# Thresholded attention: two heads per step in a hand-ordered software pipeline, with paired loads and a ones column in V

## The chip, the cores and the metric

One core of one Trainium2 chip. The metric is the device time of one execution in microseconds (us). Runs within 1.5% of the fastest of the same kernel on the same chip are called fast, and ratios use fast runs alone.

## The reference

Batch 8, 12 heads, 512 positions, head size 64, all fp32, threshold 0.1:

```python
scores = einsum('bhqd,bhkd->bhqk', Q, K) * scale
weights = exp(scores - max(scores))
weights = weights / (sum(weights) + 1e-10)
weights = where(weights > threshold, weights, 0)
weights = weights / (sum(weights) + 1e-10)
return einsum('bhqk,bhkd->bhqd', weights, V)
```

Both kernels leave out the maximum, and compare exp(score) with 0.1 times the sum of its row rather than divide first. So a row needs two sums: that of all exps (for the threshold) and that of the exps kept (for the division at the end).

## The kernel before

Per batch it loads Q, K and V whole, repacks Q and K on ScalarE so that two heads lie side by side (128 columns), and transposes each pair, so that the even head of a pair lies on partitions 0 to 63 and the odd one on 64 to 127. Then it goes head by head, and in each head by tiles of 128 queries, which I call slices; there are 8 x 12 x 4 = 384. The order on the engines is left to the scheduler.

```python
for hp in range(HP):                                   # repacking
    nc.scalar.mul(q_dst[:, hp], q_src[:, hp], 1.0)
    nc.scalar.mul(k_dst[:, hp], k_src[:, hp], 1.0)
...                                                    # cut: fp32 transposes of pairs, copied out by ScalarE
for h in range(H):
    pslc = slice(h2 * 64, (h2 + 1) * 64)               # cut: h2 = h % 2
    ...
    for qi in range(SO):
        nc.tensor.matmul(sc[:], lhsT=qt_h[:, qi, :], rhs=kt_h, start=True, stop=True)
        nc.scalar.activation(exp_sb[:], sc[:], Exp, scale=scale, accum_out=sum1[:])
        nc.vector.tensor_scalar_mul(tv[:], sum1[:], thr)
        nc.vector.scalar_tensor_tensor(                # the mask
            out=masked[:], in0=exp_sb[:], scalar=tv[:], in1=exp_sb[:],
            op0=is_gt, op1=mult, accum_out=sum2[:])
        nc.vector.tensor_scalar_add(sum2[:], sum2[:], 1e-10)
        nc.vector.reciprocal(rcp2[:], sum2[:])
        for kj in range(SO):                           # cut: four bf16 transposes, masked -> pt_ps
        nc.vector.tensor_copy(pt_sb[:], pt_ps[:])
        for kj in range(SO):                           # cut: four value matmuls, pt_sb x v -> ops
        nc.vector.tensor_scalar_mul(out_sb[:, h, qi, :], ops[:], rcp2[:])
```

The softmax here doesn't subtract the row's maximum and nothing guards it: scores larger than these inputs give would overflow.

## Time and profile before

| kernel before | value |
|---|---|
| time, three runs | 711.37 us median (699.3 to 713.16) |
| busy share: TensorE, VectorE, ScalarE | 94%, 81%, 51% |
| one slice on TensorE, undisturbed | 1.50 us |
| stretches at half clock | 24 us from about 169; 3.4 us three times; from about 664 to the end |

In the profile lines PE is TensorE, PEld its loading of weights, DVE VectorE, ACT ScalarE and POOL GpSimd; L104 is a line of the kernel. The prediction below reads the engine shares, the chain (the work that ended last, followed back) and TensorE's timeline.

### The profile page before, as it was taken

What the parts mean: (1) busy time and instruction counts of PE and PEld (TensorE: products, weight loads), DVE (VectorE), ACT (ScalarE), POOL (GpSimd) and SP (SyncE); (2) the same over time, 40 slices, a digit from 0 to 9 for tenths busy, and PEclk for the clock granted to TensorE, in tenths of its full rate; (3) what the DMA queues carried; (4) which work ended last, traced back from release to release, by engine and by line L of the source; (5) the groups of instructions that cost most, each with busy time, mean ns of one, the idle gap of its engine ahead of it and who ended that gap; (6) DMA issues with size and microseconds to landing.
All of it is one profiled execution on the core that took longest, in us unless ns stands there. A gap on an engine that the chain in (4) does not pass through costs nothing.

```text
span 710.7 us, 12702 instructions
## 1 busy us (share of the span) xinstructions
PE 669.9 (94%) x4224; PEld 313.0 (44%) x4224; DVE 576.8 (81%) x2696; ACT 363.9 (51%) x961; POOL 1.1 (0%) x8
## 2 busy tenths in 40 slices
PE   2999999999999999999999999999999999999993
PEld 1544454443454445344454445444454444444442
DVE  0588898887588889888898989888898898888664
ACT  5663458443385346843476445844476345544320
POOL 0000000000000000000000000000000000000000
PEclk9999999997599999999999999999999999999655
DMA  9750006500055000730047000650023000200002
GB/s 304 228 178 1 1 2 190 167 1 1 1 178 178 2 1 14 246 98 1 1 130 227 1 2 1 188 168 1 1 69 111 1 1 1 90 0 1 1 0 90
DMA packets 49730, 51.14 MB, mean 72 GB/s; under 512 B 512, under 2 KB 49664, under 8 KB 49664
## 3 DMA queue, kind: packets, MB, share of 16 engines
q1 hardware_dynamic: 49664, 50.33, 22.3%
q8 instruction: 33, 0.54, 0.3%
q14 instruction: 33, 0.27, 0.1%
HBM read 37.75 MB, written 12.58 MB: 71 GB/s over the span
## 4 chain that ended last, share of the span: by engine, by line
PE 86%; DVE 5%; ACT 4%; issue 3%; DMA 2%; ACTq 0%; SPq 0%
PE sc L104 56%; PE pt_ps L125 14%; PE ops L133 9%; PE ps L90 7%; ACT exp_sb L107 3%; DVE out_sb L135 2%; DMA k_sb<-in_K_dram 2%; DVE masked L115 1%; DVE pt_sb L130 1%; ACT k_hp L82 1%; ACT qt L92 1%; DVE rcp L122 0%; DVE sum L121 0%; ACT q_hp L81 0%; DVE tv L112 0%
## 5 line engine op out<-in xcount | busy, mean ns | idle before, releaser
L104 PE MATMUL sc<-kt,qt 64*128 64x512 f32 x768 | 446.0, 675 | 11.6 <-ACT exp_sb L107 10.7
L107 ACT ACTIVATE exp_sb<-sc 128x512 f32<-128x512 f32 x384 | 229.4, 597 | 307.0 <-DVE masked L115 160.5
L115 DVE SCALAR_TENSOR_TENSOR masked<-exp_sb,tv 128x512 bf16<-128x512 f32 x384 | 282.1, 740 | 0.2
L130 DVE COPY pt_sb<-pt_ps 128x512 bf16<-128x512 bf16 x384 | 158.7, 414 | 45.3 <-PE pt_ps L125 43.3
L125 PE MATMUL pt_ps<-identity_bf,masked 128*128 128x128 bf16 x1536 | 163.9, 229 | 2.7 <-DVE masked L115 1.8
L125 PEld LDWEIGHTS <-masked 128*128 128x128 bf16 x1536 | 98.9, 101 | 150.2 <-DVE sum L121 82.6
L135 DVE TENSOR_SCALAR out_sb<-ops,rcp 128x64 f32<-128x64 f32 x384 | 108.2, 282 | 58.2 <-PE ops L133 52.8
L133 PEld LDWEIGHTS <-pt_sb 128*128 128x128 bf16 x1536 | 78.6, 100 | 165.3 <-DVE rcp L122 41.7
L104 PEld LDWEIGHTS sc<-kt,qt 64*128 64x128 f32 x768 | 116.5, 193 | 51.9 <-ACT exp_sb L107 19.9
L133 PE MATMUL ops<-v_bf,pt_sb 128*128 128x64 bf16 x1536 | 112.8, 198 | 3.8 <-DVE pt_sb L130 1.0
L107 ACT ACTIVATION_READ_ACCUMULATOR exp_sb<-sc 128x1 f32 x384 | 75.2, 196 | 0.0
L122 DVE RECIPROCAL rcp<-sum 128x1 f32<-128x1 f32 x384 | 59.4, 155 | 0.1
L121 DVE TENSOR_SCALAR sum<-sum 128x1 f32<-128x1 f32 x384 | 54.7, 143 | 0.0
L90 PE MATMUL ps<-identity_f,q_hp 128*128 128x128 f32 x192 | 38.2, 300 | 11.2 <-ACT q_hp L81 8.6
L112 DVE TENSOR_SCALAR tv<-sum 128x1 f32<-128x1 f32 x384 | 39.5, 143 | 6.4 <-ACT exp_sb L107 6.4
L90 PE MATMUL ps<-identity_f,k_hp 128*128 128x128 f32 x192 | 33.9, 292 | 4.5 <-ACT k_hp L82 3.3
L92 ACT ACTIVATE qt<-ps 128x512 f32<-128x512 f32 x48 | 28.6, 597 | 13.7 <-PE ps L90 8.2
L81 ACT ACTIVATE q_hp<-q_sb 128x512 f32<-128x512 f32 x48 | 29.4, 625 | 5.8 <-DMA q_sb<-in_Q_dram 5.8
L115 DVE DVE_READ_ACCUMULATOR masked<-exp_sb,tv 128x1 f32 x384 | 31.7, 82 | 0.0
L90 PEld LDWEIGHTS ps<-identity_f,q_hp 128*128 128x128 f32 x192 | 22.5, 149 | 17.6 <-issue 11.6
L92 ACT ACTIVATE kt<-ps 128x512 f32<-128x512 f32 x48 | 28.5, 594 | 2.8 <-PE ps L90 2.8
L82 ACT ACTIVATE k_hp<-k_sb 128x512 f32<-128x512 f32 x48 | 29.5, 625 | 0.8 <-DMA k_sb<-in_K_dram 0.8
(11 smaller groups left out, 40.0 us busy)
## 6 DMA issues: line engine op xcount, KB each, us to landing
q_sb<-in_Q_dram SPq DMA_DIRECT2D x8, 1536.0 KB, 7.1
k_sb<-in_K_dram SPq DMA_DIRECT2D x8, 1536.0 KB, 10.7
v_sb<-in_V_dram SPq DMA_DIRECT2D x8, 1536.0 KB, 10.1
out_dram<-out_sb SPq DMA_DIRECT2D x8, 1536.0 KB, 6.9
```

Source lines behind the costliest of these rows:

```text
L90: nc.tensor.matmul(ps[:, r, :], lhsT=src[:, hp, r, :], rhs=identity_f32[:], is_transpose=True, start=True, stop=True)
L92: nc.scalar.mul(dst[:, hp, :, :], ps[:], 1.0)
L104: nc.tensor.matmul(sc[:], lhsT=qt_h[:, qi, :], rhs=kt_h, start=True, stop=True)
L107: nc.scalar.activation(exp_sb[:], sc[:], mybir.ActivationFunctionType.Exp, scale=scale, accum_out=sum1[:],)
L112: nc.vector.tensor_scalar_mul(tv[:], sum1[:], thr)
L115: nc.vector.scalar_tensor_tensor(out=masked[:], in0=exp_sb[:], scalar=tv[:], in1=exp_sb[:], op0=mybir.AluOpType.is_gt, op1=mybir.AluOpType ...
L121: nc.vector.tensor_scalar_add(sum2[:], sum2[:], 1e-10)
L122: nc.vector.reciprocal(rcp2[:], sum2[:])
L125: nc.tensor.matmul(pt_ps[:, kj, :], lhsT=masked[:, kj * P:(kj + 1) * P], rhs=identity_bf[:], is_transpose=True, start=True, stop=True)
L130: nc.vector.tensor_copy(pt_sb[:], pt_ps[:])
L133: nc.tensor.matmul(ops[:], lhsT=pt_sb[:, kj, :], rhs=v_h[:, kj, :], start=(kj == 0), stop=(kj == SO - 1))
L135: nc.vector.tensor_scalar_mul(out_sb[:, h, qi, :], ops[:], rcp2[:])
```

## The change

The unit becomes a group: one tile of 128 queries of both heads of a pair. There are 192 groups, four to a pair of heads, 48 pairs.

- Both scores of a group are issued one right behind the other. Their operands lie on partitions 0 to 63 and 64 to 127, so they use two row groups of the array.
- V gets a 65th column of ones, so that the value matmul also gives the sum of the exps kept. The mask needs no accumulator, and add, reciprocal and scaling are done once per pair.
- The threshold product and the cast of V go to GpSimd. Half of the copies of transposed probabilities, now of 1024 columns, go to ScalarE.
- Q and K are loaded pair by pair straight into the paired layout, four pairs ahead. ScalarE's repacking goes; the pieces of Q and K in DRAM shrink from 1 KB to 256 bytes.
- Every instruction stays in program order (`keep`), and the program order is a pipeline: scores of group g, transposes of g-2, value matmuls of g-3.

```diff
+    def paired(ap):
+        return ap.rearrange("b (hp h2) (p r) d -> (b hp) p r h2 d", h2=2, p=P, r=SO)
+    keep = tc.keep_in_program_order
...
+        v_one = consts.tile([P, 2, SO, DV], bf16, name=f"v_one{i}")
+        nc.gpsimd.memset(v_one[:, :, :, D:DV], 1.0)
...
-        for hp in range(HP):
-            nc.scalar.mul(q_dst[:, hp], q_src[:, hp], 1.0)
-            nc.scalar.mul(k_dst[:, hp], k_src[:, hp], 1.0)
...
+    def do_qk(g):
+        hp, qi = divmod(g, SO)
+        for h2 in range(2):
+            sc = spsum.tile([P, SO * P], f32)
+            ps = slice(h2 * D, (h2 + 1) * D)
+            keep(nc.tensor.matmul(sc[:], lhsT=q_t[hp][ps, qi * P:(qi + 1) * P],
+                                  rhs=k_t[hp][ps, :], start=True, stop=True))
...
-                nc.vector.tensor_scalar_mul(tv[:], sum1[:], thr)
+        keep(nc.gpsimd.tensor_scalar(tv[:], sum1[:], thr, 1.0, op0=ALU.mult, op1=ALU.mult))
...
-                    accum_out=sum2[:],
-                nc.vector.tensor_scalar_add(sum2[:], sum2[:], 1e-10)
-                nc.vector.reciprocal(rcp2[:], sum2[:])
...
+    def do_out(hp):                       # once per pair
+        keep(nc.vector.tensor_scalar_add(rcp[:], ops[:, :, :, D:DV]..., 1e-10))
+        keep(nc.vector.reciprocal(rcp[:], rcp[:]))
+        for h2 in range(2):
+            keep(nc.vector.tensor_tensor(out=out_sb[:, h2], in0=ops[:, h2, :, 0:D],
+                in1=rcp[:, h2, :].unsqueeze(2).to_broadcast([P, SO, D]), op=ALU.mult))
...
+    for g in range(G + 4):                # conditions for the first and last groups cut
+        do_qk(g)
+        do_pt(g - 2)
+        tr = do_tr(nxt, "q" if qi == 1 else "k")     # in two groups of four
+        do_pv(g - 3)
+        do_exp(g)
+        do_trev(nxt, "q" if qi == 1 else "k", tr)
+        do_mask(g - 1)
+        do_ptev(g - 2, "act" if g % 2 else "dve")
+        do_out((g - 3) // SO)                        # at the end of a pair
```

More of the change, by code (lines that the diff above doesn't have):

```diff
@@ L5 @@
 from concourse import bass_utils, mybir
-from concourse.masks import make_identity
 from concourse._compat import with_exitstack
@@ L25 @@
     HP = H // 2
+    NP = B * HP
+    DV = D + 1
     scale = 1.0 / float(D) ** 0.5
@@ L29 @@
     bf16 = mybir.dt.bfloat16
+    ALU = mybir.AluOpType
+    keep = tc.keep_in_program_order
     def flat(ap):
-        return ap.rearrange("b h (p r) d -> b p h r d", p=P, r=SO)
-    Qf = flat(Q); Kf = flat(K); Vf = flat(V); Of = flat(out)
+        return ap.rearrange("b (hp h2) (p r) d -> (b hp) p h2 r d", h2=2, p=P, r=SO)
+    def paired(ap):
+        return ap.rearrange("b (hp h2) (p r) d -> (b hp) p r h2 d", h2=2, p=P, r=SO)
+    Qf, Kf, Vf, Of = paired(Q), paired(K), flat(V), flat(out)
     consts = ctx.enter_context(tc.tile_pool(name="consts", bufs=1))
-    identity_bf = consts.tile([P, P], bf16)
-    nc.gpsimd.memset(identity_bf[:], 0.0)
-    nc.gpsimd.affine_select(
-        out=identity_bf[:], in_=identity_bf[:],
-        compare_op=mybir.AluOpType.not_equal, fill=1.0,
-        base=0, pattern=[[-1, P]], channel_multiplier=1,
-    )
     identity_f32 = consts.tile([P, P], f32)
@@ L47 @@
         out=identity_f32[:], in_=identity_f32[:],
-        compare_op=mybir.AluOpType.not_equal, fill=1.0,
+        compare_op=ALU.not_equal, fill=1.0,
         base=0, pattern=[[-1, P]], channel_multiplier=1,
     )
-    load_pool = ctx.enter_context(tc.tile_pool(name="load", bufs=1))
-    cast_pool = ctx.enter_context(tc.tile_pool(name="cast", bufs=1))
-    t_pool = ctx.enter_context(tc.tile_pool(name="t", bufs=1))
-    tpsum = ctx.enter_context(tc.tile_pool(name="tpsum", bufs=2, space=bass.MemoryType.PSUM))
-    spsum = ctx.enter_context(tc.tile_pool(name="spsum", bufs=2, space=bass.MemoryType.PSUM))
+    identity_bf = consts.tile([P, P], bf16)
+    nc.gpsimd.tensor_copy(identity_bf[:], identity_f32[:])
+    NV = 3
+    v_bufs = []
+    for i in range(NV):
+        v_one = consts.tile([P, 2, SO, DV], bf16, name=f"v_one{i}")
+        nc.gpsimd.memset(v_one[:, :, :, D:DV], 1.0)
+        v_bufs.append(v_one)
+    load = ctx.enter_context(tc.tile_pool(name="load", bufs=6))
+    tpool = ctx.enter_context(tc.tile_pool(name="t", bufs=3))
+    spsum = ctx.enter_context(tc.tile_pool(name="spsum", bufs=4, space=bass.MemoryType.PSUM))
     ptpsum = ctx.enter_context(tc.tile_pool(name="ptpsum", bufs=2, space=bass.MemoryType.PSUM))
@@ L59 @@
     work = ctx.enter_context(tc.tile_pool(name="work", bufs=4))
-    small = ctx.enter_context(tc.tile_pool(name="small", bufs=16))
-    outp = ctx.enter_context(tc.tile_pool(name="out", bufs=2))
-    for b in range(B):
-        q_sb = load_pool.tile([P, H, SO, D], f32)
-        k_sb = load_pool.tile([P, H, SO, D], f32)
-        v_sb = load_pool.tile([P, H, SO, D], f32)
-        nc.sync.dma_start(out=q_sb[:], in_=Qf[b])
-        nc.sync.dma_start(out=k_sb[:], in_=Kf[b])
-        nc.sync.dma_start(out=v_sb[:], in_=Vf[b])
-        v_bf = cast_pool.tile([P, H, SO, D], bf16)
-        nc.vector.tensor_copy(v_bf[:], v_sb[:])
-        q_hp = cast_pool.tile([P, HP, SO, 2 * D], f32)
-        k_hp = cast_pool.tile([P, HP, SO, 2 * D], f32)
-        q_src = q_sb[:].rearrange("p (hp h2) r d -> p hp r h2 d", hp=HP)
-        k_src = k_sb[:].rearrange("p (hp h2) r d -> p hp r h2 d", hp=HP)
-        q_dst = q_hp[:].rearrange("p hp r (h2 d) -> p hp r h2 d", h2=2)
-        k_dst = k_hp[:].rearrange("p hp r (h2 d) -> p hp r h2 d", h2=2)
-        for hp in range(HP):
-            nc.scalar.mul(q_dst[:, hp], q_src[:, hp], 1.0)
-            nc.scalar.mul(k_dst[:, hp], k_src[:, hp], 1.0)
-        qt = t_pool.tile([P, HP, SO, P], f32)
-        kt = t_pool.tile([P, HP, SO, P], f32)
-        for hp in range(HP):
-            for src, dst in ((q_hp, qt), (k_hp, kt)):
-                ps = tpsum.tile([P, SO, P], f32)
-                for r in range(SO):
-                    nc.tensor.matmul(ps[:, r, :], lhsT=src[:, hp, r, :], rhs=identity_f32[:],
-                                     is_transpose=True, start=True, stop=True)
-                nc.scalar.mul(dst[:, hp, :, :], ps[:], 1.0)
-        out_sb = outp.tile([P, H, SO, D], f32)
-        for h in range(H):
-            hp = h // 2
-            h2 = h % 2
-            pslc = slice(h2 * 64, (h2 + 1) * 64)
-            qt_h = qt[pslc, hp, :, :]
-            kt_h = kt[pslc, hp, :, :].rearrange("d a b -> d (a b)")
-            v_h = v_bf[:, h, :, :]
-            for qi in range(SO):
-                sc = spsum.tile([P, SO * P], f32)
-                nc.tensor.matmul(sc[:], lhsT=qt_h[:, qi, :], rhs=kt_h, start=True, stop=True)
-                exp_sb = work.tile([P, SO * P], f32)
-                sum1 = small.tile([P, 1], f32)
-                nc.scalar.activation(
-                    exp_sb[:], sc[:], mybir.ActivationFunctionType.Exp,
-                    scale=scale, accum_out=sum1[:],
-                )
-                tv = small.tile([P, 1], f32)
-                nc.vector.tensor_scalar_mul(tv[:], sum1[:], thr)
-                masked = work.tile([P, SO * P], bf16)
-                sum2 = small.tile([P, 1], f32)
-                nc.vector.scalar_tensor_tensor(
-                    out=masked[:], in0=exp_sb[:], scalar=tv[:], in1=exp_sb[:],
-                    op0=mybir.AluOpType.is_gt, op1=mybir.AluOpType.mult,
-                    accum_out=sum2[:],
-                )
-                rcp2 = small.tile([P, 1], f32)
-                nc.vector.tensor_scalar_add(sum2[:], sum2[:], 1e-10)
-                nc.vector.reciprocal(rcp2[:], sum2[:])
-                pt_ps = ptpsum.tile([P, SO, P], bf16)
-                for kj in range(SO):
-                    nc.tensor.matmul(pt_ps[:, kj, :],
-                                     lhsT=masked[:, kj * P:(kj + 1) * P],
-                                     rhs=identity_bf[:], is_transpose=True,
-                                     start=True, stop=True)
-                pt_sb = work.tile([P, SO, P], bf16)
-                nc.vector.tensor_copy(pt_sb[:], pt_ps[:])
-                ops = opsum.tile([P, D], f32)
-                for kj in range(SO):
-                    nc.tensor.matmul(ops[:], lhsT=pt_sb[:, kj, :], rhs=v_h[:, kj, :],
-                                     start=(kj == 0), stop=(kj == SO - 1))
-                nc.vector.tensor_scalar_mul(out_sb[:, h, qi, :], ops[:], rcp2[:])
-        nc.sync.dma_start(out=Of[b], in_=out_sb[:])
@@ new lines, with do_load @@
+    small = ctx.enter_context(tc.tile_pool(name="small", bufs=8))
+    outp = ctx.enter_context(tc.tile_pool(name="out", bufs=3))
+    q_in, k_in, v_in, q_t, k_t = {}, {}, {}, {}, {}
+    e_t, s_t, t_t, m_t, ptp_t, pts_t, o_t = {}, {}, {}, {}, {}, {}, {}
+    sc_t = {}
+    def do_load(hp):
+        q_sb = load.tile([P, SO, 2 * D], f32)
+        k_sb = load.tile([P, SO, 2 * D], f32)
+        v_sb = load.tile([P, 2, SO, D], f32)
+        for dst, src in ((q_sb, Qf), (k_sb, Kf)):
+            for h2 in range(2):
+                nc.sync.dma_start(out=dst[:, :, h2 * D:(h2 + 1) * D], in_=src[hp][:, :, h2, :])
+        nc.sync.dma_start(out=v_sb[:], in_=Vf[hp])
+        q_in[hp], k_in[hp], v_in[hp] = q_sb, k_sb, v_sb
@@ new lines, in do_vcast, with do_tr, do_trev @@
+    def do_vcast(hp):
+        keep(nc.gpsimd.tensor_copy(v_bufs[hp % NV][:, :, :, 0:D], v_in[hp][:]))
+    def do_tr(hp, which):
+        src = q_in[hp] if which == "q" else k_in[hp]
+        sc = spsum.tile([P, SO * P], f32)
+        for r in range(SO):
+            keep(nc.tensor.matmul(sc[:, r * P:(r + 1) * P], lhsT=src[:, r, :],
+                                  rhs=identity_f32[:], is_transpose=True, start=True, stop=True))
+        return sc
+    def do_trev(hp, which, sc):
+        if which == "q":
+            qt = tpool.tile([P, SO * P], f32)
+            keep(nc.scalar.copy(qt[:], sc[:]))
+            q_t[hp] = qt
+        else:
+            kt = tpool.tile([P, SO * P], f32)
+            keep(nc.scalar.copy(kt[:], sc[:]))
+            k_t[hp] = kt
@@ new lines, in do_qk, with do_exp @@
+    def do_qk(g):
+        hp, qi = divmod(g, SO)
+        for h2 in range(2):
+            sc = spsum.tile([P, SO * P], f32)
+            ps = slice(h2 * D, (h2 + 1) * D)
+            keep(nc.tensor.matmul(sc[:], lhsT=q_t[hp][ps, qi * P:(qi + 1) * P],
+                                  rhs=k_t[hp][ps, :], start=True, stop=True))
+            sc_t[g, h2] = sc
+    def do_exp(g):
+        exp_sb = work.tile([P, 2, SO * P], f32)
+        sum1 = small.tile([P, 2], f32)
+        for h2 in range(2):
+            keep(nc.scalar.activation(
+                exp_sb[:, h2, :], sc_t.pop((g, h2))[:], mybir.ActivationFunctionType.Exp,
+                scale=scale, accum_out=sum1[:, h2:h2 + 1],
+            ))
+        tv = small.tile([P, 2], f32)
+        keep(nc.gpsimd.tensor_scalar(tv[:], sum1[:], thr, 1.0, op0=ALU.mult, op1=ALU.mult))
+        e_t[g], t_t[g] = exp_sb, tv
@@ new lines, in do_mask, with do_pt @@
+    def do_mask(g):
+        masked = work.tile([P, 2, SO * P], bf16)
+        exp_sb, tv = e_t.pop(g), t_t.pop(g)
+        for h2 in range(2):
+            keep(nc.vector.scalar_tensor_tensor(
+                out=masked[:, h2, :], in0=exp_sb[:, h2, :], scalar=tv[:, h2:h2 + 1],
+                in1=exp_sb[:, h2, :], op0=ALU.is_gt, op1=ALU.mult,
+            ))
+        m_t[g] = masked
+    def do_pt(g):
+        masked = m_t.pop(g)
+        pt_ps = ptpsum.tile([P, 2, SO, P], bf16)
+        for h2 in range(2):
+            for kj in range(SO):
+                keep(nc.tensor.matmul(pt_ps[:, h2, kj, :], lhsT=masked[:, h2, kj * P:(kj + 1) * P],
+                                      rhs=identity_bf[:], is_transpose=True, start=True, stop=True))
+        ptp_t[g] = pt_ps
@@ new lines, in do_ptev, with do_pv @@
+    def do_ptev(g, eng):
+        pt_sb = work.tile([P, 2, SO, P], bf16)
+        if eng == "act":
+            keep(nc.scalar.copy(pt_sb[:], ptp_t.pop(g)[:]))
+        else:
+            keep(nc.vector.tensor_copy(pt_sb[:], ptp_t.pop(g)[:]))
+        pts_t[g] = pt_sb
+    def do_pv(g):
+        hp, qi = divmod(g, SO)
+        if qi == 0:
+            ops = opsum.tile([P, 2, 512], f32)
+            o_t[hp] = ops
+        ops = o_t[hp]
+        pt_sb = pts_t.pop(g)
+        for h2 in range(2):
+            for kj in range(SO):
+                keep(nc.tensor.matmul(ops[:, h2, qi * DV:(qi + 1) * DV], lhsT=pt_sb[:, h2, kj, :],
+                                      rhs=v_bufs[hp % NV][:, h2, kj, :],
+                                      start=(kj == 0), stop=(kj == SO - 1)))
@@ new lines, in do_out @@
+    def do_out(hp):
+        ops = o_t.pop(hp)[:, :, 0:SO * DV].rearrange("p h (r d) -> p h r d", d=DV)
+        rcp = small.tile([P, 2, SO], f32)
+        keep(nc.vector.tensor_scalar_add(rcp[:], ops[:, :, :, D:DV].rearrange("p h r o -> p h (r o)"), 1e-10))
+        keep(nc.vector.reciprocal(rcp[:], rcp[:]))
+        out_sb = outp.tile([P, 2, SO, D], f32)
+        for h2 in range(2):
+            keep(nc.vector.tensor_tensor(
+                out=out_sb[:, h2], in0=ops[:, h2, :, 0:D],
+                in1=rcp[:, h2, :].unsqueeze(2).to_broadcast([P, SO, D]), op=ALU.mult))
+        nc.sync.dma_start(out=Of[hp], in_=out_sb[:])
@@ new lines @@
+    PRE = 4
+    for hp in range(PRE):
+        do_load(hp)
+    do_vcast(0)
+    for w in ("q", "k"):
+        do_trev(0, w, do_tr(0, w))
+    G = NP * SO
+    for g in range(G + 4):
+        hp, qi = divmod(g, SO)
+        nxt = hp + 1
+        if g < G:
+            if qi == 0 and hp + PRE < NP:
+                do_load(hp + PRE)
+            if qi == 0 and nxt < NP:
+                do_vcast(nxt)
+            do_qk(g)
+        if 0 <= g - 2 < G:
+            do_pt(g - 2)
+        tr = None
+        if g < G and nxt < NP and qi in (1, 2):
+            tr = do_tr(nxt, "q" if qi == 1 else "k")
+        if 0 <= g - 3 < G:
+            do_pv(g - 3)
+        if g < G:
+            do_exp(g)
+        if tr is not None:
+            do_trev(nxt, "q" if qi == 1 else "k", tr)
+        if 0 <= g - 1 < G:
+            do_mask(g - 1)
+        if 0 <= g - 2 < G:
+            do_ptev(g - 2, "act" if g % 2 else "dve")
+        if g - 3 >= 0 and (g - 3) % SO == SO - 1:
+            do_out((g - 3) // SO)
```

## The prediction

> **What bounds the kernel now.** I read the page's engine shares, then the chain that ended last, then TensorE's timeline in an undisturbed stretch, then the stretches where the clock row falls. From the page, engine shares, granted clock per slice of the span, the chain by engine, and the costliest group:
>
> ```profile
> PE 669.9 (94%) x4224; PEld 313.0 (44%) x4224; DVE 576.8 (81%) x2696; ACT 363.9 (51%) x961; POOL 1.1 (0%) x8
> ...
> PEclk9999999997599999999999999999999999999655
> ...
> PE 86%; DVE 5%; ACT 4%; issue 3%; DMA 2%; ACTq 0%; SPq 0%
> ...
> L104 PE MATMUL sc<-kt,qt 64*128 64x512 f32 x768 | 446.0, 675 | 11.6 <-ACT exp_sb L107 10.7
> ```
>
> TensorE (PE) is 86% of the chain, and the fp32 score matmul (L104) is its largest part; each of the 384 score tiles is two records, two passes. TensorE's timeline, start and duration in us:
>
> ```profile
> 302.06 0.39 PE L125 MATMUL pt_ps<-identity_bf,masked 128*128 128x128 bf16 x4
> 302.37 1.12 PE L104 MATMUL sc<-kt,qt 64*128 64x512 f32 x2
> 303.43 0.23 PE L125 MATMUL pt_ps<-identity_bf,masked 128*128 128x128 bf16 x1
> 303.49 0.28 PE L133 MATMUL ops<-v_bf,pt_sb 128*128 128x64 bf16 x4
> 303.61 0.33 PE L125 MATMUL pt_ps<-identity_bf,masked 128*128 128x128 bf16 x3
> 303.87 1.12 PE L104 MATMUL sc<-kt,qt 64*128 64x512 f32 x2
> 304.93 0.34 PE L125 MATMUL pt_ps<-identity_bf,masked 128*128 128x128 bf16 x3
> 305.10 0.28 PE L133 MATMUL ops<-v_bf,pt_sb 128*128 128x64 bf16 x4
> 305.22 0.22 PE L125 MATMUL pt_ps<-identity_bf,masked 128*128 128x128 bf16 x1
> ```
>
> Durations overlap, so I use distances between starts. One slice (one head, 128 queries) repeats every 1.50 us (302.37 to 303.87), with no idle noted. The score holds the engine 1.06 us (303.87 to 304.93); three transposes take 0.17 (304.93 to 305.10), so 0.057 each; four value matmuls 0.12 (305.10 to 305.22), so 0.029 each. Four of each is 0.34, and 1.06 + 0.34 = 1.40: the missing 0.10 us lies just before the score. VectorE (DVE) is close behind: 576.8 / 384 = 1.50 us busy per slice, partly overlapping records. ScalarE (ACT) has half its time free.
>
> 384 x 1.50 = 576; the rest of the 711 is 384 fp32 input transposes, joins between batches, the start, and two stretches at half clock. In the table by stretches (PE, PEld, DVE, ACT, POOL, clock, DMA):
>
> ```profile
> 280.00:360.00 80.00, 78.18 (x516) 36.29 (x516) 69.74 (x332) 44.19 (x119) 0.00 (x0) 1.00 0.26 80
> 169.00:192.00 23.00, 23.00 (x90) 9.82 (x89) 12.04 (x59) 6.64 (x19) 0.00 (x0) 0.50 0.00 1
> 664.00:690.00 26.00, 26.00 (x100) 10.94 (x98) 14.27 (x69) 6.97 (x22) 0.00 (x0) 0.50 0.00 0
> ```
>
> The reader sees 90 matmuls in 23 us at clock 0.50, against 516 in 80 us at 1.00: 3.9 against 6.5 per us, with TensorE busy throughout. TensorE sets the rate.
>
> **What the Trainium skill says.** "TensorE: Matmul & The Clock Gate", Part 3, The mechanism, says that matmuls on different row groups run concurrently, starts about 4 ns apart. Its examples are not two-pass fp32, so I looked for one here, and found it at batch joins, where the scheduler happened to issue the last head of one batch beside the first of the next (an odd head beside an even one, so the other half of the rows). The first line below is the join before batch 2, the second the join before batch 1, where the two scores run one behind the other:
>
> ```profile
> 202.04 1.13 PE L104 MATMUL sc<-kt,qt 64*128 64x512 f32 x4
> 203.19 0.29 PE L133 MATMUL ops<-v_bf,pt_sb 128*128 128x64 bf16 x4
> ...
> 108.63 0.60 PE L90 MATMUL ps<-identity_f,k_hp 128*128 128x128 f32 x4
> 109.16 1.98 PE L104 MATMUL sc<-kt,qt 64*128 64x512 f32 x4
> 111.08 0.29 PE L133 MATMUL ops<-v_bf,pt_sb 128*128 128x64 bf16 x4
> ```
>
> Two score tiles (x4 records) finish in 1.13 us, the time of one; elsewhere the same four need 1.98. The trace agrees, also for two passes. That the fast one is two row groups is my inference; the trace has no rows. "TensorEngine Tiling (Array Packing)", Key Properties, says that changing the tiling mode drains the engine; the 0.10 us ahead of a score agrees. "TensorE: Matmul & The Clock Gate", Part 1, says that an engine that is too idle falls to half clock; the stretches above show the half clock, and also that full record-busy time did not lift it. "DMA: Bandwidth & Descriptors", Why small descriptors are slow, gives 256-byte descriptors 27% overhead; the old kernel has only 1 KB ones, so nothing in its trace shows it.
>
> **The change, part by part.** The unit is now a group: two heads, one 128-query tile; 192 groups, four to a head pair, 48 pairs.
>
> TensorE per group: two scores together 1.10 (between 1.06 and the 1.15 from 202.04 to 203.19); one drain 0.10; eight transposes 8 x 0.057 = 0.46; eight value matmuls 8 x 0.029 = 0.23 (65 columns for 64). Sum 1.89. Per pair come eight fp32 transposes, in bursts of four: (109.16 - 108.63 - 0.10) / 4 = 0.11 each, so 0.88. A pair costs 4 x 1.89 + 0.88 = 8.4 us, against 8 x 1.50 + 0.88 = 12.9 before.
>
> VectorE per pair. The exps' threshold product goes to GpSimd; the 1e-10 add, reciprocal and scaling go from 384 times each to once per pair; the masked sum's accumulator read goes (the ones column gives the sum). Left: eight masks at about 0.65 (658 ns to the accumulator read before) = 5.2; two copies of 1024 from PSUM, twice the elements of a 0.33 us one, at about 0.6 = 1.2; the output, 0.07 + 0.07 + two 256-element products at an estimated 0.4 = 1.0. Sum 7.4.
>
> ScalarE per pair. It loses the 96 repacking copies, since loads arrive paired. Eight exps at 0.58 to 0.67 between starts = 5.0; two Q/K evictions at 0.49 = 1.0; and, new, half of the probability evictions, two copies of 1024 elements at an estimated 0.92 = 1.8 (a 512 one takes 0.49 between starts). Sum 7.8.
>
> So three engines stand at 8.4, 7.8 and 7.4 per pair. The hand order gives each stage about one group of slack: score g, exp g, mask g one later, transposes two later, value product three later. I followed one period by hand: exp g starts 0.16 after its score, the mask finds its threshold in time, the output copy ends 0.3 us before the single output bank is wanted again. It just fits. For the stumbles of so tight a fit I add 0.2: 8.6 us per pair, 48 x 8.6 = 413. Ends: first loads, transposes and half clock cost more (score 1 began at 17.2 before; small loads should bring it to 10 or 11), and TensorE is cold for some 10 us, costing 6. The last groups drain through five stages and a store, 9. Sum 413 + 11 + 6 + 9 = 439.
>
> **The rivals.** (1) *The scores do not overlap.* If passes queue in order and only the middle ones overlap, a pair of scores costs three passes of 0.43, not two, 1.5 us per group, 10.1 a pair, 510 in all. Against it: the 1.13 us line. (2) *ScalarE, or the waits between the three, become the bound.* At 93% of TensorE's load, with long copies in some groups and none in others, bursts can make TensorE wait for a score bank or for the one output bank; GpSimd's unmeasured delay lies in the same loop. At 9.2 a pair: 470. (3) *Half clock.* If waits keep TensorE from counting as busy, groups cost up to 3.7 us; each 24 us spent so costs about 10. For it: the two stretches before. Against: two row groups fill the array better. Stuck throughout, about 720. (4) *Transfers.* Q and K now come in 256-byte pieces, 2048 a pair. If each took as long as a 1 KB packet (the DMA queue's share, 22.3% of 16 x 710.7 us over 49664 packets, is 51 ns), a pair would need (2048 + 512) x 51 / 16 = 8.2 us, as much as TensorE; I expect half of that, hidden behind a prefetch of four pairs.
>
> **Range and chances.** 440 as the middle. The low end, 420, is 8.3 a pair and no losses; the high end, 480, is rival 2 in full with one half-clock stretch. Rival 1 (5%) or 3 (3%) would leave it above. Even rival 1 is faster than 711; slower needs a half clock throughout. Faster by over 2%: 0.97; within 2%: 0.01; slower: 0.02.
>
> **What would show each step right or wrong.** Right: in TensorE's timeline the score rows come as x4 of about 1.13 us, one pair of heads every 8.4 to 8.7 us, VectorE and ScalarE both busy 80% or more, clock row at 9 after the start, GpSimd's rows short. Wrong: score rows of 1.5 or 2.0 (rival 1); waits of scores on exp, or of value matmuls on the output scaling, of more than some 20 us in the list of waits (rival 2); fives in the clock row (rival 3); DMA tenths at 9 and transposes waiting for loads (rival 4).

## More of the kernel before

From the page of the kernel before, the DMA queue (packets, MB, share of 16 engines) and four groups (busy us, mean ns of one, idle before them):

```profile
q1 hardware_dynamic: 49664, 50.33, 22.3%
...
L115 DVE SCALAR_TENSOR_TENSOR masked<-exp_sb,tv 128x512 bf16<-128x512 f32 x384 | 282.1, 740 | 0.2
L130 DVE COPY pt_sb<-pt_ps 128x512 bf16<-128x512 bf16 x384 | 158.7, 414 | 45.3 <-PE pt_ps L125 43.3
...
L122 DVE RECIPROCAL rcp<-sum 128x1 f32<-128x1 f32 x384 | 59.4, 155 | 0.1
L121 DVE TENSOR_SCALAR sum<-sum 128x1 f32<-128x1 f32 x384 | 54.7, 143 | 0.0
```

A reciprocal and an add of 128 single numbers cost 0.15 us each, 384 times over: work that carries almost no data.

The chip's TensorE clock is not granted in full in every execution: the run of the kernel before takes 687.6 us at a mean granted clock of 0.990 and 724.3 us at 0.931.

## The result, and the profile after

The changed kernel takes **422.7 us** (median of four runs, 422.52 to 422.9, all fast, correct). Four runs of the kernel before beside it have the median 705.34. The ratio is 0.604, with a 95% interval of 0.600 to 0.607.

From the page of the changed kernel: engine shares, granted clock, DMA queue, chain, and two groups:

```profile
PE 408.8 (97%) x4224; PEld 245.6 (58%) x4224; DVE 389.9 (93%) x672; ACT 368.7 (88%) x961; POOL 70.6 (17%) x250
...
PEclk9999999999999999999999999999999999999999
...
q1 hardware_dynamic: 127488, 50.35, 45.6%
...
PE 96%; DVE 2%; DMA 1%; SPq 0%; ACT 0%; issue 0%; DVEq 0%; ACTq 0%
...
L131 DVE SCALAR_TENSOR_TENSOR masked<-exp_sb,tv 128x512 bf16<-128x512 f32 x384 | 290.1, 796 | 22.7 <-POOL tv L124 13.2
...
L111 PE MATMUL sc<-kt,qt 64*128 64x512 f32 x768 | 218.3, 646 | 0.7 <-ACT kt L103 0.7
```

TensorE has as many matmuls as before (4224), and the score group's busy time falls from 446.0 to 218.3 us, though the mean record is hardly shorter (646 ns for 675): two of them run at the same time. VectorE has 672 instructions for 2696. The chain is TensorE's for 96%. All three engines are at 88% or more, and the clock row has no five.

TensorE's timeline of the changed kernel (start, duration, count), with the start of each of the five groups from one pair to the next:

```profile
199.95 1.13 PE L111 MATMUL sc<-kt,qt 64*128 64x512 f32 x4
201.02 0.62 PE L142 MATMUL pt_ps<-identity_bf,masked 128*128 128x128 bf16 x8
201.47 0.42 PE L163 MATMUL ops<-v_one,pt_sb 128*128 128x65 bf16 x8
201.82 1.13 PE L111 MATMUL sc<-kt,qt 64*128 64x512 f32 x4
...
203.75 1.13 PE L111 MATMUL sc<-kt,qt 64*128 64x512 f32 x4
...
206.06 1.13 PE L111 MATMUL sc<-kt,qt 64*128 64x512 f32 x4
...
208.38 1.13 PE L111 MATMUL sc<-kt,qt 64*128 64x512 f32 x4
```

A pair of scores holds the engine 1.07 us (199.95 to 201.02). The pair of heads takes 208.38 - 199.95 = 8.43 us, and over the steady part of the trace 8.424 on average. 48 x 8.42 = 404; the other 18 us are the ends: the first score begins at 7.87, at half speed until about 12.5, the last record of a score begins at 410.2, and the span ends at 420.7.

How near the others come, in the table by stretches (length, then busy us of PE, PEld, DVE, ACT, POOL, then clock, DMA share, GB/s):

```profile
200.00:240.00 40.00, 40.00 (x419) 24.16 (x420) 38.67 (x68) 36.17 (x97) 6.92 (x24) 1.00 0.49 129
```

VectorE is busy 38.67 / 40 x 8.43 = 8.15 us per pair, ScalarE 7.6. VectorE stands higher than the 7.4 of the prediction. Part of the reason is a line of the timeline of the changed kernel's VectorE, beside one of its GpSimd:

```profile
201.26 3.38 DVE L131 SCALAR_TENSOR_TENSOR masked<-exp_sb,tv 128x512 bf16<-128x512 f32 x4
```
```profile
202.82 0.61 POOL L86 CAST v_one<-v_sb 128x512 bf16<-128x512 f32 x1
```

Four masks in which GpSimd's cast of V falls take 3.38 us; the next four, without one, take 2.90. One mask of each pair lasts 1.18 us in place of 0.74.

So the questions to the chip are these. Is it the two row groups that give TensorE its gain, or only the tighter order? Would the gain have come without VectorE's relief, without the hand order, or without the paired loads? And what binds at 8.42: TensorE alone (my theory), VectorE (the rival), or the loop of waits between them?

### The profile page after: what moved, and what is told of

Its sections match the earlier page's. It is cut to its first block, busy times and chain, and to the rows that moved or that the text cites. A ratio compares the mean times of both kernels' runs of the same rounds, so it can differ in the third digit from the quotient of the medians.

```text
span 420.7 us, 11494 instructions
## 1 busy us (share of the span) xinstructions
PE 408.8 (97%) x4224; PEld 245.6 (58%) x4224; DVE 389.9 (93%) x672; ACT 368.7 (88%) x961; POOL 70.6 (17%) x250
## 3 DMA queue, kind: packets, MB, share of 16 engines
q1 hardware_dynamic: 127488, 50.35, 45.6%
## 4 chain that ended last, share of the span: by engine, by line
PE 96%; DVE 2%; DMA 1%; SPq 0%; ACT 0%; issue 0%; DVEq 0%; ACTq 0%
PE sc L111 48%; PE pt_ps L142 25%; PE ops L163 12%; PE sc L92 10%; DVE masked L131 1%; DMA k_sb<-in_K_dram 1%; SPq L81 0%; DVE out_sb L174 0%; ACT pt_sb L149 0%; DVE pt_sb L151 0%; ACT kt L103 0%; DVE rcp L171 0%; DVEq L243 0%; DVE rcp L170 0%; ACTq L149 0%
## 5 line engine op out<-in xcount | busy, mean ns | idle before, releaser
L111 PE MATMUL sc<-kt,qt 64*128 64x512 f32 x768 | 218.3, 646 | 0.7 <-ACT kt L103 0.7
L142 PE MATMUL pt_ps<-identity_bf,masked 128*128 128x128 bf16 x1536 | 119.4, 220 | 0.8 <-DVE masked L131 0.8
L149 ACT COPY pt_sb<-pt_ps 128x1024 bf16<-128x1024 bf16 x96 | 98.2, 1023 | 2.0 <-PE pt_ps L142 2.0
L124 POOL TENSOR_SCALAR tv<-sum 128x2 f32<-128x2 f32 x192 | 39.7, 207 | 330.6 <-ACT exp_sb L119 181.0
L163 PE MATMUL ops<-v_one,pt_sb 128*128 128x65 bf16 x1536 | 81.5, 194 | 1.3 <-DVE out_sb L174 0.5
L111 PEld LDWEIGHTS sc<-kt,qt 64*128 64x128 f32 x768 | 58.4, 186 | 13.1 <-ACT kt L103 1.1
L151 DVE COPY pt_sb<-pt_ps 128x1024 bf16<-128x1024 bf16 x96 | 65.4, 681 | 0.0
L174 DVE TENSOR_TENSOR out_sb<-ops,rcp 128x256 f32<-128x256 f32 x96 | 36.3, 420 | 1.9 <-DVE rcp L171 0.3
L92 PE MATMUL sc<-identity_f,q_sb 128*128 128x128 f32 x192 | 30.1, 280 | 4.7 <-DMA q_sb<-in_Q_dram 4.7
L86 POOL CAST v_one<-v_sb 128x512 bf16<-128x512 f32 x48 | 29.8, 621 | 10.8 <-DMA v_sb<-in_V_dram 7.9
```

What stands on the lines that cost most here:

```text
L86: keep(nc.gpsimd.tensor_copy(v_bufs[hp % NV][:, :, :, 0:D], v_in[hp][:]))
L92: keep(nc.tensor.matmul(sc[:, r * P:(r + 1) * P], lhsT=src[:, r, :], rhs=identity_f32[:], is_transpose=True, start=True, stop=True))
L111: keep(nc.tensor.matmul(sc[:], lhsT=q_t[hp][ps, qi * P:(qi + 1) * P], rhs=k_t[hp][ps, :], start=True, stop=True))
L124: keep(nc.gpsimd.tensor_scalar(tv[:], sum1[:], thr, 1.0, op0=ALU.mult, op1=ALU.mult))
L142: keep(nc.tensor.matmul(pt_ps[:, h2, kj, :], lhsT=masked[:, h2, kj * P:(kj + 1) * P], rhs=identity_bf[:], is_transpose=True, start=True, s ...
L149: keep(nc.scalar.copy(pt_sb[:], ptp_t.pop(g)[:]))
```

## The experiments

Eleven kernels ran. The table has the median of all runs of a kernel; for same_rows, split_scores and before_pairs these include slow ones, which the ratio leaves out. "Wrong" marks kernels whose output is wrong; all others were correct.

| run | time, us | ratio to before |
|---|---|---|
| changed kernel | 422.7 | 0.604 |
| same_rows (wrong) | 595.8 | 0.846 |
| split_scores | 638.3 | 0.907 |
| old_dve_work | 693.8 | 0.986 |
| old_dve_spread | 575.6 | 0.822 |
| no_keep | 525.5 | 0.747 |
| act_repack | 438.8 | 0.627 |
| half_value (wrong) | 420.4 | 0.601 |
| accum_mask | 423.4 | 0.605 |
| half_value_cast_act (wrong) | 414.2 | 0.592 |
| quick_start | 423.2 | 0.605 |
| before_pairs | 699.5 | 0.985 |

### Is it the row groups? same_rows

Both scores of a group read partitions 0 to 63, so the second head's score is computed from the first head's data. Count, sizes and order of instructions stay.

```diff
-            ps = slice(h2 * D, (h2 + 1) * D)
+            ps = slice(0, D)
```

> Both scores of a group read rows 0 to 63, so the odd head's result is wrong on purpose; order and counts stay. Theory (two row groups are what lets the scores overlap): four passes run one behind the other, as in the old kernel's slow join, 1.92 us from score to next matmul in place of 1.06, so +0.86 per group, 3.4 per pair, 8.43 + 3.4 = 11.9, in all 48 x 11.9 + 18 = 588 us, score rows x4 of about 1.98 us. Rival (any two adjacent scores overlap, the rows do not matter): 423 us. If the clock falls to half in some stretches although TensorE has no idle time, the row groups matter for the clock as well.

Measured 595.84 us (593.92 to 604.71, four runs, one of them slow). TensorE's timeline of same_rows, early in the run (the first two rows) and in the steady state:

```profile
37.82 3.78 PE L111 MATMUL sc<-kt,qt 64*128 64x512 f32 x4
...
43.78 2.10 PE L111 MATMUL sc<-kt,qt 64*128 64x512 f32 x4
...
199.69 1.98 PE L111 MATMUL sc<-kt,qt 64*128 64x512 f32 x4
201.60 0.62 PE L142 MATMUL pt_ps<-identity_bf,masked 128*128 128x128 bf16 x8
```

The scores hold TensorE 1.91 us (199.69 to 201.60) where they held it 1.07. That is the row groups shown: nothing else in the program differs. 192 x 0.84 = 161 us, which makes 584; the other 12 have another cause, which the first two rows show. TensorE ran at about half speed (3.78 us) until 43.8 us into the run; the changed kernel left that at about 12.5. By the two durations, 31 us of it cost some 15. Why the slow start lasts longer here is open; all four runs lie some 10 us or more above 584, so it probably is no accident of the one run that was profiled. The table by stretches prints the clock as 1.00 in that time, but only because the trace's clock record has no entry there: its first one, at full clock, begins at 44.1 us (at 12.5 in the changed kernel).

### Must they be adjacent? split_scores

The second head's score is issued after the first four transposes, and everything else stays.

```diff
-            do_qk(g)
+            do_qk(g, (0,))
         if 0 <= g - 2 < G:
-            do_pt(g - 2)
+            do_pt(g - 2, between=lambda: do_qk(g, (1,)))    # after four of the eight transposes
```

> The second head's score comes after the first four probability transposes; everything else as it was. Theory: adjacency is needed, each score costs its own 1.06 us and its own 0.10 of drain, so +1.16 per group, 4.6 per pair: 48 x 13.1 + 18 = 645 us. Rival (TensorE's look-ahead brings them together, or another engine bounds the kernel): 423 to 450 us.

Measured 638.34, 637.87 and 638.39 us. TensorE's timeline of split_scores:

```profile
202.37 1.12 PE L111 MATMUL sc<-kt,qt 64*128 64x512 f32 x2
203.43 0.40 PE L144 MATMUL pt_ps<-identity_bf,masked 128*128 128x128 bf16 x4
...
204.01 1.12 PE L111 MATMUL sc<-kt,qt 64*128 64x512 f32 x2
```

Each score now takes 1.06 by itself, as in the kernel before, and pays the drain of 0.1 us again. So two row groups are of no use here when transposes on all 128 rows stand between their matmuls. A fourth run took 1151.51 us with a recorded clock of 0.999. It had no profile. I leave it out of the comparison, and come back to it in the last section.

### Would the order and the pairs have done without VectorE's relief? old_dve_work and old_dve_spread

old_dve_work has the new order and the paired scores, but gives VectorE its old work: threshold, accumulated sum, add, reciprocal and scaling per slice, all copies and the V cast. With the scaling per slice the output bank changes too: one per group, two of them, in place of one per pair. The parts of the relief are taken back together; what each is worth was not tested.

```diff
-        keep(nc.gpsimd.tensor_scalar(tv[:], sum1[:], thr, 1.0, op0=ALU.mult, op1=ALU.mult))
+            keep(nc.vector.tensor_scalar_mul(tv[:], sum1[:, h2:h2 + 1], thr))          # per head
-                in1=exp_sb[:, h2, :], op0=ALU.is_gt, op1=ALU.mult,
+                in1=exp_sb[:, h2, :], op0=ALU.is_gt, op1=ALU.mult, accum_out=sum2[:],
+            keep(nc.vector.tensor_scalar_add(sum2[:], sum2[:], 1e-10))
+            keep(nc.vector.reciprocal(rcp2[:], sum2[:]))
...
+            keep(nc.vector.tensor_scalar_mul(ob_t[hp][:, h2, qi, :], ops[:, h2, 0:D], rcps[h2][:]))
```

> The new order and the paired scores, but VectorE does the old work: threshold product, accumulated second sum, add, reciprocal, scaling per slice, all probability copies, V's cast. Theory (TensorE's gain is only there because VectorE was relieved with it): VectorE needs 8 x 1.42 + 0.3 less a little for the wider copies, about 11.5 us per pair, so 48 x 11.5 + 18 = 570 us with VectorE busy over 93% and TensorE near 75%. Rival (VectorE had enough slack, its relief is a trimming): below 450 us.

Measured 693.77 us (693.52 to 694.13): a miss by 124. The timeline of VectorE in old_dve_work shows where it lies:

```profile
300.02 0.08 DVE L136 DVE_READ_ACCUMULATOR masked<-exp_sb,tv 128x1 f32 x1
300.14 0.15 DVE L140 TENSOR_SCALAR sum<-sum 128x1 f32<-128x1 f32 x1
300.33 0.16 DVE L141 RECIPROCAL rcp<-sum 128x1 f32<-128x1 f32 x1
300.41 0.13 DVE L135 TENSOR_SCALAR tv<-sum 128x1 f32<-128x1 f32 x1
300.58 0.75 DVE L136 SCALAR_TENSOR_TENSOR masked<-exp_sb,tv 128x512 bf16<-128x512 f32 x1
```

The threshold product follows 0.08 us behind the reciprocal, on which it does not depend. The add that needs the accumulator's value starts 0.12 behind its read, the reciprocal 0.19 behind the add that it needs, the mask 0.17 behind the threshold that it needs. In the kernel before, the scheduler had put other slices' work between such steps: there a mask starts 0.06 us behind an add that it does not need (302.85 and 302.91 in its trace). My sum had taken that distance for all of them.

If that is the cause, the same work with other instructions between such steps must be fast. old_dve_spread does both thresholds first, and the adds and reciprocals after the copy (the edit is against old_dve_work):

```diff
+        for h2 in range(2):
+            keep(nc.vector.tensor_scalar_mul(tvs[h2][:], sum1[:, h2:h2 + 1], thr))
         for h2 in range(2):
             keep(nc.vector.scalar_tensor_tensor(...))
-            keep(nc.vector.tensor_scalar_add(sum2[:], sum2[:], 1e-10))
-            keep(nc.vector.reciprocal(rcp2[:], sum2[:]))
+    def do_rcp(g):       # called after the copy of group g - 2
+        for h2 in range(2): keep(nc.vector.tensor_scalar_add(sums[h2][:], sums[h2][:], 1e-10))
+        for h2 in range(2): keep(nc.vector.reciprocal(rcps[h2][:], sums[h2][:]))
```

> As old_dve_work, but no small VectorE operation directly follows the one it depends on: both thresholds first, the adds and reciprocals after the copy. If the 0.12 to 0.19 us ahead of each dependent small operation was what made old_dve_work 694 us in place of 570, this comes to about 11.5 us per pair, 48 x 11.5 + 15 = 567 us. If it was something else (the masks themselves, or the reach of the one-group delay), it stays above 650.

Measured 575.57 us (575.36 to 575.75), 118 less for the same 2544 instructions of VectorE. The table by stretches of old_dve_spread has VectorE as the bound, and TensorE waiting:

```profile
200.00:300.00 100.00, 82.44 (x751) 43.35 (x750) 100.00 (x456) 53.48 (x156) 0.00 (x0) 1.00 0.34 92
```

So VectorE's old work costs 11.7 us per pair in the better of the two orders tried. With it the paired scores end at 576, not 423.

### Is the hand order needed? no_keep

The same program, with the scheduler free.

```diff
-    keep = tc.keep_in_program_order
+    keep = lambda made: made
```

> The same program with the scheduler free to reorder. In the built kernel 147 of the 192 score pairs are still adjacent on TensorE, 45 have value matmuls between. Theory: each separated pair costs 1.16 us, 52 us, so about 475 us, if the rest of the order is as good. Rival (the order matters little): 423 to 430 us. If the scheduler's other moves hurt, above 500.

Measured 525.52 us (524.57 to 526.0). The built order has 147 of the 192 pairs of scores adjacent; by the estimate before the run the 45 separated ones cost 52 us, which makes 475. The other 50 us are waits, and some half clock. From the list of waits of no_keep (total us, times, longest), from its page, and from its timeline of TensorE:

```profile
PE ops L163 <- DVE out_sb L174: 40.7, 47, 1.0
...
PEclk9999999899999899999899999989999998999999
```
```profile
302.17 1.12 PE L111 MATMUL sc<-kt,qt 64*128 64x512 f32 x2
304.21 0.43 PE L163 MATMUL ops<-v_one,pt_sb 128*128 128x65 bf16 x8 [0.91 <-DVE out_sb L174]
304.57 1.12 PE L111 MATMUL sc<-kt,qt 64*128 64x512 f32 x2
```

Once per pair, a value matmul has been brought ahead of the second score, and waits for the single output bank until VectorE has read it. It holds up the score behind it, which was ready. That is 40.7 us of idle TensorE. The eights in the clock row are five stretches of 3.4 us at half clock, some 8 us more (an estimate from the ratio of the two speeds in same_rows, 1.9). So the order is worth 103 us: 52 for adjacency, 41 for not putting a waiting instruction in front of a ready one, and the rest mostly the clock.

### Are the paired loads needed? act_repack

Loads in pieces of 1 KB, and ScalarE packs Q and K again, one copy of 512 columns each per pair.

```diff
-    Qf, Kf, Vf, Of = paired(Q), paired(K), flat(V), flat(out)
+    Qf, Kf, Vf, Of = flat(Q), flat(K), flat(V), flat(out)
+    def do_pack(hp, which):
+        packed = tpool.tile([P, SO, 2 * D], f32)
+        keep(nc.scalar.copy(packed[:].rearrange("p r (h2 d) -> p r h2 d", h2=2),
+                            src[hp][:].rearrange("p h2 r d -> p r h2 d")))
```

> Q and K come in whole 1 KB rows as before the change, and ScalarE packs them, two copies of 512 a pair at 0.52: ScalarE goes from 7.6 to 8.65 us per pair. If it then bounds: 430 to 436 us. If the paired loads' real cost was in the 256-byte transfers, this is faster than 423. If neither matters: 423. The DMA queue's share should fall from 45.6% to under 30% in each case.

Measured 438.84 us (438.53 to 439.1), a little above the expectation: ScalarE becomes the bound. The table by stretches of act_repack has ScalarE at 98.94 of 100 us, and its page the DMA queue:

```profile
200.00:300.00 100.00, 100.00 (x1009) 59.94 (x1008) 93.96 (x160) 98.94 (x252) 16.16 (x58) 1.00 0.41 120
```
```profile
q1 hardware_dynamic: 52224, 50.34, 38.2%
```

The paired loads are worth 16 us, because they spare ScalarE: it is busy 7.6 of 8.42 us per pair with them, and the whole period without. The DMA share fell only from 45.6% to 38.2%, where I had expected under 30%: the small pieces are cheap. A packet of 256 bytes takes 18 ns in the trace of the changed kernel (median and mean), one of 1 KB 46 (median) to 51 (mean).

### What binds at 8.42 us per pair? half_value, accum_mask, half_value_cast_act

half_value takes half of the value matmuls away (0.46 us per pair on TensorE); accum_mask loads VectorE with an unread accumulated sum.

```diff
-            for kj in range(SO):          # half_value: value matmuls
+            for kj in range(2):
```
```diff
+                accum_out=sum2[:, h2:h2 + 1],      # accum_mask: in the mask of the changed kernel
```

> Value matmuls over two of the four key blocks only, wrong on purpose: TensorE loses 16 x 0.029 = 0.46 us per pair, VectorE, ScalarE and the waits stay. If TensorE alone sets the time: 8.43 - 0.46 = 7.97 per pair, 423 - 22 = 401 us. If VectorE (93% busy, 8.1 us per pair) stands right behind it: 408 to 412 us with VectorE at 96% or more. If some wait that goes round all engines sets the pace: 423 us.

> The masks also accumulate a second sum that nobody reads: 384 accumulator reads more on VectorE, 0.05 to 0.08 us each, 0.4 to 0.6 per pair. If VectorE has its 4% of slack and no more, it becomes the bound at 8.5 to 8.7 per pair: 427 to 436 us. If its slack in the waits is larger than its busy share tells: 423 us.

half_value measured 420.35 us (420.11 to 420.7, six runs): 8.375 per pair in its trace, of the 0.46 only 0.05. (quick_start, below, ran on the same chip with the changed kernel's steady order, and has 8.424 there too.) From its table by stretches and its list of waits:

```profile
200.00:300.00 100.00, 97.24 (x859) 56.12 (x858) 97.14 (x167) 92.24 (x241) 30.19 (x60) 1.00 0.48 127
```
```profile
PE ops L163 <- DVE out_sb L174: 11.0, 45, 0.7
```

TensorE is no longer busy throughout, and waits once per pair for VectorE to empty the output bank. So a second bound stands only 0.05 us behind TensorE: VectorE's work and the loop over the output bank. Two things keep this from being a clean measure. By distances between starts VectorE's own work in the changed kernel is 8.04 us per pair (worked out under "Why the prediction was right"); the other 0.38 it waits, before two of the eight masks, for GpSimd's threshold product. So the bound is a loop through VectorE and not its work alone. And half_value shifts that loop: GpSimd's products, 0.19 us in the changed kernel, take 0.40 in it (medians), and GpSimd is busy 30% where it was 17%.

accum_mask measured 423.43 us (422.67 to 424.0), but does not count as a test. The masks start 0.673 us apart with the accumulator and 0.663 without: its read costs 0.010 us each, 384 times, so VectorE was loaded with 4 us in all, far less than I meant. Whether VectorE had slack stays undecided by it.

half_value_cast_act also gives GpSimd's V cast to ScalarE, to see whether the stretched mask is part of that second bound.

```diff
-        keep(nc.gpsimd.tensor_copy(v_bufs[hp % NV][:, :, :, 0:D], v_in[hp][:]))
+        keep(nc.scalar.copy(v_bufs[hp % NV][:, :, :, 0:D], v_in[hp][:]))
```

> half_value again (wrong on purpose), with V's cast moved from GpSimd to ScalarE. In the changed kernel one mask per pair lasts 1.18 us in place of 0.74, the one that runs beside the cast. Theory (VectorE is the second bound, and the cast beside it is a part of its load): VectorE falls from 8.4 to 7.7 us per pair, TensorE stands at 7.97, ScalarE rises from 7.6 to 8.1; the slowest of them sets 8.1 to 8.2, 406 to 412 us, and no mask lasts over 0.8 us. Rival (half_value stays at 420 because of a wait that goes round the engines, not because of VectorE's load): 420 us.

Measured 414.2 us (413.82 to 414.7), 8.224 per pair; a little over the window that I gave. The masks (minimum, median, maximum in ns) in the changed kernel, then in half_value_cast_act:

```profile
L131 DVE SCALAR_TENSOR_TENSOR masked<-exp_sb,tv x384: 732/745/1182, 11.6 to 413.7; 128x512 bf16<-128x512 f32 x192
```
```profile
L131 DVE SCALAR_TENSOR_TENSOR masked<-exp_sb,tv x384: 739/746/758, 12.9 to 404.9; 128x512 bf16<-128x512 f32 x192
```

No mask is over 758 ns now, and 6 us are gone: the cast on GpSimd did stretch a mask per pair, and that was part of the second bound. Probably it ends there because ScalarE, busy 98.78 of 100 us, is next; this was not tested. TensorE binds the changed kernel: it has no idle time between the first score and the last. The loop through VectorE stands less than 1% behind it, as far as half_value tells, and ScalarE some 10% (7.6 of 8.42).

### Two tries at a better or a cheaper version: quick_start, before_pairs

quick_start warms TensorE with 12 idle transposes while the first loads run, and issues the first K loads from ScalarE.

```diff
+    for _ in range(3):                   # 12 transposes of the identity
+        warm = spsum.tile([P, SO * P], f32, name="sc")
...
+            eng = nc.scalar if hp == 0 and dst is k_sb else nc.sync
```

> A version meant to be kept: twelve idle transposes of the identity warm TensorE while the first loads travel, and the first K loads are issued by ScalarE beside SP's Q loads. Clock: full from about 6 us, not 12.5; first score at 6 to 7 us, not 7.9. Expected 418 to 420 us, against 422.7. If the start is hidden by something later, 422.7.

Measured 423.16 us (420.87 to 423.77, seven runs): no gain. The trace shows TensorE at full speed from its first real transpose (its clock record begins at full clock at 4.7 us, when nothing but the idle transposes had run), yet the first score begins at 7.39 for 7.87: the loads and ScalarE's copy set the start. The profiled span is 419.0 for 420.7, and the other runs show nothing of it.

before_pairs is the kernel before with only the program order changed: both heads' scores of a tile next to each other, the scheduler free.

```diff
-        for h in range(H):               # head, then query tile
+        for hp in range(HP):             # pair, then query tile: both scores, then the rest of each head
+            for qi in range(SO):
+                for h2 in range(2):
+                    nc.tensor.matmul(sc[:], lhsT=qt_h[:, qi, :], rhs=kt_h, start=True, stop=True)
```

> The kernel before, its program order changed alone: both heads' scores of a query tile are written next to each other, the scheduler is left free. In the built kernel only 8 of the 192 pairs are adjacent on TensorE (10 score matmuls happened to be adjacent before). Theory (adjacency in the built order is what pays, and it does not come from program order): 695 to 715 us, as before. Rival (interleaving two heads helps by itself, more independent work): below 680 us.

Measured 688.6 and 689.63 us in the fast runs, 709.37 and 765.21 in slow ones; the ratio of the fast runs is 0.985 (0.976 to 0.995). Part of that is the clock: these two runs had 0.98, while the fast runs of the kernel before took 697 to 698 us at 0.97 and 687.62 at 0.99. In the order as built only 8 of the 192 pairs stayed adjacent. Asking for pairs without holding the order gives almost nothing. None of the eleven beats the changed kernel with a correct result.

## Why the prediction was right

- **TensorE per group.** Worked out as 8.4 us per pair, measured 8.42. The inference from one line at a batch join, that two scores on two row groups cost the time of one, holds: 1.07 us for two, and same_rows takes it back. It was less of a gamble than one line looks: the trace of the kernel before has ten places with two scores side by side, three at 1.13 us, three at 2.08 to 2.22 in stretches of half clock, and four at 1.98.
- **The allowance for stumbles,** 0.2 us per pair or 10 us in all, was not needed: the fit by hand was right, TensorE has no idle time from the first score to the last.
- **The ends.** 26 us predicted, 18.4 measured. The first score begins at 7.87 and not at 11. The cold stretch, priced at 6, costs nothing that can be seen: counted from the first score to the last a pair takes 8.41, no more than in the steady part. The emptying at the end is as predicted (8.5 for 9), and 1.9 us of the measured time lie outside the span. This term (7.6) and the allowance (48 x (8.6 - 8.424) = 8.5) make up the 16 us between the sum of 439 and 422.7.
- **VectorE.** 7.4 predicted, 8.15 measured: the term was too small. By distances between starts it is 8.04: a mask per pair that GpSimd's cast stretches adds 0.44; the other masks stand 0.663 apart and not 0.65 (the 658 ns read from the kernel before are near the shortest there, 657 to 679 with a median of 667), which adds 0.1; and the output takes 1.10 and not 1.0, because its first steps stand 0.19 and 0.24 apart where I took 0.07, while the two products take 0.67 and not 0.8. The margin to the next bound was 0.05 us in half_value, not the 1.0 that the sums promised. The prediction did not work out so thin a margin: that TensorE and not this loop set the time was in part luck.
- **ScalarE.** 7.8 predicted, 7.6 busy. The long copy was priced right (0.92 assumed, 0.90 between starts; its record is 1.02 long), and the exps stand at the low end of their assumed 0.58 to 0.67 (0.59 from 201.16 to 201.75).
- **Rival 1** (no overlap) is refuted: same_rows shows what no overlap looks like. Its price, 510, assumed that the middle passes overlap; with none of that left it is 596, some 12 of them slow start. **Rival 2** (the waits) did not come about, but no_keep shows it: 525 with the same instructions. **Rival 3** (half clock) did not come about in any run of the changed kernel. **Rival 4** (transfers) did not come about: a packet of 256 bytes takes 18 ns where 1 KB takes 46 to 51, and the transfers stay hidden, as expected.
- **What the prediction did not say:** it set only TensorE's two sums against each other, 12.9 and 8.4, and did not price the parts one by one. The runs show three conditions, each of which is needed: without the row groups 596, without VectorE's relief 576 to 694, without the hand order 525. They do not add up to the gain, since each takes away a different bound.

## What to carry to other kernels

Here two matmuls whose operands fill half of the rows each cost the time of one (1.07 us) when they lay on different halves and were neighbours in TensorE's queue, and not otherwise (1.91 on the same half, 1.06 each when parted); a single line of the old trace can show whether it works for the type at hand. Such a gain is only had if the next engine is relieved too, so add up all engines per period before changing one. Keep short steps apart from what they depend on. In a tight pipeline hold the order by hand, and put no instruction that will wait in front of one that is ready.

## What the Trainium skill lacked or had wrong

- **"TensorE: Matmul & The Clock Gate", Part 3, The mechanism,** does not say whether matmuls of two passes overlap too. The runs show that two-pass fp32 matmuls overlap on two row groups as well: both first passes start 7 ns apart, then both second ones, and two 64-row scores take 1.13 us where they take 1.98 on the same rows.
- **The same page, Part 1,** ties the half clock to idle time. Here TensorE stayed slow while its records show it busy all the time: over 20 us twice in the kernel before, and same_rows, which differs from the changed kernel only in the rows used, left its slow start at 43.8 us rather than about 12.5. More filled rows alone do not explain it: same_rows after its start, and split_scores, whose scores each fill 64 rows by themselves, held full speed to the end. In quick_start twelve transposes were enough to leave the slow start (full clock from 4.7 us). What decides stays open. The clock record has no entry before the slow start ends, so a recorded mean of 0.999 does not exclude a slow run. The run of split_scores at 1151.51 us may have been one that stayed at half speed throughout (a group of same_rows took 5.12 us in its slow start and 2.73 after, a ratio of 1.88; 1151.51 / 638.3 is 1.80), but it has no profile: this stays open.
- **"TensorEngine Tiling (Array Packing)", Key Properties,** gives no size for the drain; here about 0.10 us lie ahead of a score with 64 rows.
- **"VectorE: DVE Perf Modes", The DRAIN you can't avoid,** says of a series of copies that "the semaphore costs nothing extra here". For short instructions here it does matter whether one depends on the one before: 0.12 to 0.19 us between starts against 0.08, and 694 against 576 us for a kernel full of them. An accumulator read behind a mask of 512 costs 0.010 us from start to start in accum_mask; no page has it.
- **"SBUF — State Buffer", Who interferes with whom,** says that a VectorE instruction with two SBUF inputs contends with a GpSimd instruction that reads SBUF. The trace agrees and adds a size: a mask goes from 0.74 to 1.18 us beside a cast of 0.61.
- **"DMA: Bandwidth & Descriptors", Why small descriptors are slow,** gives 27% overhead at 256 bytes: 3 of 11 cycles, which by the same formula (3 of 35 at 1 KB) makes 1.26 times the cost per byte. Here 18 ns for a packet of 256 bytes against 46 to 51 for 1 KB is 1.4 to 1.6 times, and the whole queue's share rose only from 38.2% to 45.6%: more than the page says, but no reason to avoid such pieces where an engine's copy is saved.
